# A two-layer encoder trunk: the last chunks of each down-projection product move into another buffer ring, and the last product ends in another order

## The chip, the cores and the metric

The kernel runs on one core of a Trainium2 chip. The metric is device time in microseconds (us), the median over several executions. The engines are TensorE (PE, with its weight loads as PEld), VectorE (DVE), ScalarE (ACT), GpSimd (POOL) and SyncE (SP), which issues the DMAs of this kernel.

## What is computed

An encoder trunk of two layers on 1024 tokens of width 1024, everything in float32. Each layer mixes tokens (windowed attention in the first, neighbourhood attention in the second, both beside heads that attend to 256 memory tokens), and then runs a gated feed-forward part. The change lies in the last two lines:

```python
gu = jnp.einsum('bsd,df->bsf', h, w_gu[i])
f = jnp.einsum('bsf,fd->bsd', jax.nn.silu(gu[..., :D_FF]) * gu[..., D_FF:], w_down[i])
x = x + rms_norm(f, norm_ffn_post[i])
```

D_FF is 2816, so the down projection multiplies a 1024x2816 matrix by a 2816x1024 one, and its rows are then scaled to unit mean square, multiplied by a gain and added to x.

## The kernel before

Every float32 operand is split into a high part that TensorE takes as it is (ScalarE copies it, L1118) and the rest (VectorE subtracts, L1120), and every product is three matmuls (`mm3`, L90 to L93): high x high, high x rest, rest x high.

The down projection is computed by blocks, two by two, with **seven products** of half size in place of eight, so that sums of blocks stand on either side. The sums are prepared in the gate and up stage and lie in HBM (`act_d`, `both_d`). Each product (`product4`, L1124) multiplies a 512x1408 block by a 1408x512 block: 11 chunks m of 128 inner rows, times four row tiles t, times three matmuls of 128x512, so 132 matmuls. The seven calls stand at the end of the stage; I number them 1 to 7 in program order. Products 2, 5, 6 and 7 end in a step on rows: `first_half`, `done_first` (L1157 adds, `part`, `finish`), `second_half`, `done_second`.

`operands` (L1103) gets chunk m: one DMA of 512 KB (L1117), or two of 256 KB (L1114, L1115), into a tile `draw`; then the high part `dh` on ScalarE (L1118) and the rest `dl` on VectorE (L1120). These tiles come from the pool `dp` with three buffers of each. In product 1 the first four chunks (`EARLY`) use `ring` instead, the pool through which the weights of the projections pass (two raw buffers `wr`, three of each part, `wh` and `wl`), because `dp` opens only when the stage before has ended.

`product4` runs chunks 0 to 8 with t inside. The last two (`GROUP`) are kept, and then run with t outside, so that the four accumulators end one after the other and `post(t)` follows each. PSUM holds eight accumulators, so the next product starts at once.

`part(t, k)` squares one half of a row tile on ScalarE with an accumulator (L1174) and multiplies the half by the gain on GpSimd (L1175). `finish(t, half)` adds the two sums of squares (L161), raises to the power -0.5 on GpSimd (L165), does one `scalar_tensor_tensor` on VectorE over 128x1024 (L1181) and stores the row tile (512 KB, L422 or L424). In the first layer it goes on with the next layer's norm; `turn_some` then transposes four row tiles on TensorE during product 6 (L186, eight matmuls of 128x128 each).

The order on each engine and on SP's queue is set by the framework: it takes instructions by priority, which is program order, as their inputs and buffers come ready by its own timing model, so that an instruction can stand ahead of earlier ones whose buffers are not free. Each queue then runs in that fixed order. The weights of the second layer's first projection come through `ring` too, after the down projection in program order (L105, L115, L116).

Of the kernel before, what the change touches and what calls it, by code (L numbers as in the profile page):

```python
# [12 lines left out]
ALU = mybir.AluOpType  # L13
# [10 lines left out]
HALF = 512  # L24
DFF = 2816
NF = DFF // P
FH = NF // 2
# [9 lines left out]
GROUP = 2  # L37
# [6 lines left out]
LEAD, EARLY = 6, 4  # L44
# [22 lines left out]
def build(nc, tc, ctx, x_in, mem_in, wts, t5, onehot, sinks, rpb, maskb, gains, out):  # L67
# [18 lines left out]
    dma = nc.sync  # L86
# [3 lines left out]
    def mm3(ps, lh, ll, rh, rl, start, stop):  # L90
        nc.tensor.matmul(ps, lh, rh, start=start, stop=False)  # L91
        nc.tensor.matmul(ps, lh, rl, start=False, stop=False)  # L92
        nc.tensor.matmul(ps, ll, rh, start=False, stop=stop)  # L93
# [14 lines left out]
    def unit_tiles(u, pl, n, tag=""):  # L108
        return [pl.tile([P, 1024], F32R, name=f"w{k}{u}", tag=f"w{k}{tag}", bufs=n) for k in "hl"]
# [48 lines left out]
    def rms(npool, parts):  # L158
        ms = npool.tile([P, 1], F32, name="ms", bufs=4)
        if len(parts) == 2:  # L160
            nc.vector.scalar_tensor_tensor(ms, parts[0], EPS, parts[1], ALU.add, ALU.add)  # L161
        else:
            nc.vector.tensor_scalar(ms, parts[0], EPS, None, ALU.add)
        r = npool.tile([P, 1], F32, name="r", bufs=4)
        nc.gpsimd.tensor_tensor(r, ms, mhalf, ALU.pow)  # L165
        return r

    def gain(npool, k, tag):
        g = npool.tile([P, D], F32, name=f"g_{k}", tag=tag)
        dma.dma_start(out=g, in_=gains[k:k + 1, :].broadcast_to([P, D]))  # L170
        return g
# [229 lines left out]
    def grid_rows(ap, j):  # L401
        return ap.rearrange("(r c) d -> c r d", c=COLS)[8 * j:8 * j + 8]
# [17 lines left out]
    def store_x(dst, t, i, grid):  # L420
        if grid:
            dma.dma_start(out=grid_rows(dst, i), in_=t)  # L422
        else:
            dma.dma_start(out=dst[i * P:(i + 1) * P, :], in_=t)  # L424
# [195 lines left out]
    for layer in range(DEPTH):  # L620
        windowed = layer == 0
        last = layer == DEPTH - 1
# [207 lines left out]
        gpost = gain(npool, DEPTH + layer, "g0")  # L830
# [48 lines left out]
        def load_xt(i):  # L879
            t = npool.tile([P, D], F32, name="xt", bufs=2)  # L880
            load_x(t, x_cur, i, layer == 0)
            return t
# [12 lines left out]
        for i in range(NT):  # L895
            accs = [psO.tile([P, HALF], F32, name="acc", tag="acc") for _ in range(2)]
            now_ao, ao = ao, heads_out(i + 1) if i < NT - 1 else None
            xt = load_xt(i)
# [75 lines left out]
        def add(o, a, b):  # L974
            nc.vector.tensor_tensor(o, a, b, ALU.add)  # L975
# [82 lines left out]
        for n, ((tH, tL), (b, t)) in enumerate(((T2, (1, 1)), (T1, (0, 0)), (T3, (0, 1)), (T4, (1, 0)))):  # L1058
            for i in range(4):
                eng = nc.gpsimd if (n, i) in TPOOL else nc.vector  # L1060
# [35 lines left out]
        x_next = out if last else x_scr[1]  # L1096
        held = []

        def turn_held():
            i, ht = held.pop(0)  # L1100
            turn(psD, "acc", ht, split_into(hH, hL, i))

        def operands(a, both, w):  # L1103
            def get(m):
                if a == 0 and m < EARLY:
                    raw = ring.tile([P, D], F32, name="draw", tag="wr", bufs=2)
                    h, lo = unit_tiles(f"d{m}", ring, 3)
                else:
                    raw = dp.tile([P, D], F32, name="draw", tag="draw", bufs=DRAW)
                    h, lo = (dp.tile([P, D], F32R, name=f"d{k}", tag=f"d{k}", bufs=DRAW) for k in "hl")  # L1110
                if both is None:
                    u = U_DN + NF * layer + m + (FH if w else 0)
                    ws = slice(HALF, D) if w == 2 else slice(0, HALF)
                    dma.dma_start(out=raw[:, :HALF], in_=act_d[layer][a, m])  # L1114
                    dma.dma_start(out=raw[:, HALF:], in_=wts[u, :, ws])  # L1115
                else:
                    dma.dma_start(out=raw, in_=both_d[layer][both, m])  # L1117
                nc.scalar.activation(h, raw, AF.Copy)  # L1118
                eng = nc.gpsimd if (both, m) in DPOOL else nc.vector
                eng.tensor_tensor(lo, raw, h.bitcast(F32), ALU.subtract)  # L1120
                return h, lo
            return get

        def product4(get, post, between=None, group=GROUP):  # L1124

            accs = [psD.tile([P, HALF], F32, name="acc", tag="acc") for _ in range(4)]

            def step(t, m, h, lo):
                ts = slice(t * P, (t + 1) * P)
                mm3(accs[t], h[:, ts], lo[:, ts], h[:, HALF:], lo[:, HALF:], m == 0, m == FH - 1)  # L1130

            kept = []
            for m in range(FH):
                hl = get(m)
                if m < FH - group:
                    for t in range(4):
                        step(t, m, *hl)
                else:
                    kept.append((m, hl))
                if between:  # L1140
                    between(m)
            for t in range(4):
                for m, hl in kept:
                    step(t, m, *hl)
                post(t, accs[t])
# [8 lines left out]
        tts, xts, sss = [], [], []  # L1154
# [12 lines left out]
                load_x(xt, x_new, 4 * half + t, False)  # L1167
                xts.append(xt)

        def part(t, k):  # L1170

            ks = slice(k * HALF, (k + 1) * HALF)
            junk = npool.tile([P, HALF], F32, name="junk", bufs=2)
            nc.scalar.activation(junk, tts[t][:, ks], AF.Square, scale=ROOT, accum_out=sss[t][:, k:k + 1])  # L1174
            nc.gpsimd.tensor_tensor(tts[t][:, ks], tts[t][:, ks], gpost[:, ks], ALU.mult)  # L1175

        def finish(t, half):
            i = 4 * half + t
            r = rms(npool, [sss[t][:, 0:1], sss[t][:, 1:2]])
            xt, tt = xts[t], tts[t]  # L1180
            nc.vector.scalar_tensor_tensor(xt, tt, r, xt, ALU.mult, ALU.add)  # L1181
            store_x(x_next, xt, i, last)
            if not last:
                ss = npool.tile([P, 1], F32, name="ss", bufs=4)
                nc.scalar.activation(tt, xt, AF.Square, scale=ROOT, accum_out=ss)
                r = rms(npool, [ss])
                nc.vector.scalar_tensor_tensor(tt, xt, r, gpre, ALU.mult, ALU.mult)
                held.append((i, tt))

        def first_half(t, ps):  # L1190
            add(tts[t][:, :HALF], ps, U[t])
            part(t, 0)

        def done_first(t, ps):
            add(tts[t][:, HALF:], ps, V[t])
            part(t, 1)
            finish(t, 0)

        def second_half(t, ps):
            if t == 0:  # L1200
                next_rows(1)
                load_xts(1)
            add(tts[t][:, HALF:], ps, V[t])
            add(U[t], ps, U[t])
            part(t, 1)

        def done_second(t, ps):
            add(tts[t][:, :HALF], ps, U[t])
            part(t, 0)
            finish(t, 1)  # L1210

        def turn_some(m):
# [2 lines left out]

        next_rows(0)
        product4(operands(0, None, 0), lambda t, ps: nc.scalar.activation(U[t], ps, AF.Copy))
        gpost = gain(npool, 4 * DEPTH + layer, "g0")
        product4(operands(1, None, 1), first_half)
        gpre = None if last else gain(npool, layer + 1, "g1")  # L1220
        load_xts(0)
        product4(operands(None, 3, None), lambda t, ps: add(U[t], ps, U[t]))
        product4(operands(None, 0, None), lambda t, ps: add(V[t], ps, U[t]))
        product4(operands(2, None, 2), done_first)
        product4(operands(None, 1, None), second_half, turn_some)
        while not last and held:
            turn_held()
        product4(operands(None, 2, None), done_second)
        dph.close()
        ops.close()  # L1230
        if last:
# [89 lines left out]
```

## Time and profile before

| | |
|---|---|
| median of 3 runs | 2269.01 us (2265.79 to 2272.14) |
| the profiled execution | 2261.95 us |
| its span, first to last instruction | 2260.2 us |
| mean granted TensorE clock in it | 0.983 of full |
| TensorE matmul busy | 2141.8 us, 95% |
| VectorE busy | 1513.8 us, 67% |
| ScalarE busy | 1064.9 us, 47% |
| GpSimd busy | 726.2 us, 32% |
| DMA, mean | 149 GB/s |

The down projection of the first layer lies at about 888 to 1112 us of the span, that of the second at 2020 to 2242 us. The 7 us between the profiled execution and the median lie outside the profile, so sums are made against 2261.95 us and moved to the median at the end.

### The profile page before, as it was taken

What the parts mean: (1) busy time and instruction counts of PE and PEld (TensorE: products, weight loads), DVE (VectorE), ACT (ScalarE), POOL (GpSimd) and SP (SyncE); (2) the same over time, 40 slices, a digit from 0 to 9 for tenths busy, and PEclk for the clock granted to TensorE, in tenths of its full rate; (3) what the DMA queues carried; (4) which work ended last, traced back from release to release, by engine and by line L of the source; (5) the groups of instructions that cost most, each with busy time, mean ns of one, the idle gap of its engine ahead of it and who ended that gap; (6) DMA issues with size and microseconds to landing.
All of it is one profiled execution on the core that took longest, in us unless ns stands there. A gap on an engine that the chain in (4) does not pass through costs nothing. (4 is left out here: it accounts for less than half of the span.)

```text
span 2260.2 us, 31296 instructions
## 1 busy us (share of the span) xinstructions
PE 2141.8 (95%) x10538; PEld 1779.4 (79%) x10538; DVE 1513.8 (67%) x2629; ACT 1064.9 (47%) x2162; POOL 726.2 (32%) x810
## 2 busy tenths in 40 slices
PE   7899888989999999999899999999899999999986
PEld 7678787768888888887788889777688888888865
DVE  5578785588777765556657665765877777755556
ACT  5488784442233333534457665754523333224333
POOL 3167661424333321102215342524233333211012
PEclk9999999999999999999999999999999999999998
DMA  6433445325555544856333232433255545446664
GB/s 206 118 88 91 135 135 156 98 79 189 175 183 170 180 138 162 276 193 235 114 104 97 78 87 69 132 112 107 75 180 183 184 170 177 145 146 222 193 207 164
DMA packets 152791, 336.49 MB, mean 149 GB/s; under 512 B 24727, under 2 KB 47127, under 8 KB 152632
## 3 DMA queue, kind: packets, MB, share of 16 engines
q1 hardware_dynamic: 152632, 334.50, 46.2%
q8 instruction: 84, 1.38, 0.3%
q14 instruction: 75, 0.61, 0.1%
HBM read 229.06 MB, written 95.03 MB: 143 GB/s over the span
## 5 line engine op out<-in xcount | busy, mean ns | idle before, releaser
L975 DVE TENSOR_TENSOR zt<-acc,zt 128x512 f32<-128x512 f32 x300 | 204.9, 686 | 155.9 <-PE acc L93 153.7
L1120 DVE TENSOR_TENSOR dl<-draw,dh 128x1024 fp32r<-128x1024 f32 x146 | 187.1, 1288 | 163.7 <-ACT dh L1118 163.1
L274 POOL TENSOR_TENSOR sn<-sn,st 128x384 f32<-128x384 f32 (+1 forms) x256 | 188.1, 736 | 254.3 <-DVE st L273 217.7
L1118 ACT ACTIVATE dh<-draw 128x1024 fp32r<-128x1024 f32 x146 | 154.0, 1059 | 218.5 <-PE acc L93 125.8
L92 PE MATMUL acc<-dl,dh 128*128 128x512 f32 x584 | 229.7, 393 | 14.9 <-DVE dl L1120 13.0
L93 PE MATMUL acc<-dh,dl 128*128 128x512 f32 x584 | 228.2, 391 | 0.0
L91 PE MATMUL acc<-dh 128*128 128x512 f32 x584 | 225.3, 391 | 1.3 <-ACT dh L1118 1.2
L918 ACT ACTIVATE gh<-zt 128x512 fp32r<-128x512 f32 x168 | 104.4, 628 | 175.7 <-PE acc L92 156.8
L994 POOL TENSOR_TENSOR tw<-tw 128x512 f32<-128x512 f32 x88 | 131.9, 1499 | 119.1 <-DMA tw<-in_wts 114.2
L1175 POOL TENSOR_TENSOR tt<-tt,g 128x512 f32<-128x512 f32 x32 | 52.2, 1643 | 363.9 <-ACT junk L1174 310.8
L116 DVE TENSOR_TENSOR wl<-wr,wh 128x1024 fp32r<-128x1024 f32 x92 | 118.2, 1285 | 67.3 <-ACT wh L115 65.5
L994 POOL TENSOR_TENSOR zt<-zt 128x512 f32<-128x512 f32 x66 | 90.3, 1368 | 205.1 <-DVE zt L972 201.7
L91 PE MATMUL psg<-hH,wh 128*128 128x512 f32 x384 | 153.1, 399 | 1.8 <-DVE k L229 1.4
L971 ACT ACTIVATE zt<-zt 128x512 f32<-128x512 f32 x84 | 53.1, 632 | 214.7 <-DVE zt L975 214.7
L115 ACT ACTIVATE wh<-wr 128x1024 fp32r<-128x1024 f32 x100 | 105.5, 1055 | 100.5 <-DMA wr<-in_wts 74.9
L92 PE MATMUL psg<-hL,wh 128*128 128x512 f32 x384 | 152.8, 398 | 0.0
L93 PE MATMUL psg<-hH,wl 128*128 128x512 f32 x384 | 152.5, 397 | 0.0
L292 PE MATMUL psv<-PT,v 128*128 128x256 f32 x656 | 143.0, 319 | 5.0 <-DVE attn L667 3.8
L98 DVE TENSOR_TENSOR PT<-pst,PT 128x384 fp32r<-128x384 f32 (+1 forms) x256 | 126.8, 495 | 29.7 <-ACT PT L97 25.1
L92 PEld LDWEIGHTS acc<-dl,dh 128*128 128x128 f32 x584 | 110.0, 188 | 43.3 <-DVE dl L1120 20.7
L272 ACT ACTIVATE sn<-sn,st 128x385 f32<-128x385 f32 (+3 forms) x192 | 113.0, 588 | 60.0 <-DVE st L269 55.7
L920 DVE TENSOR_TENSOR gl<-zt,gh 128x512 fp32r<-128x512 f32 x168 | 129.8, 775 | 7.5 <-ACT gh L918 7.5
(231 smaller groups left out, 5960.1 us busy)
## 6 DMA issues: line engine op xcount, KB each, us to landing
wr<-in_wts SPq DMA_DIRECT2D x146, 512.0 KB
draw<-both_d SPq DMA_DIRECT2D x88, 512.0 KB
both_d<-zt SPq DMA_DIRECT2D x88, 256.0 KB
tw<-in_wts SPq DMA_DIRECT2D x44, 512.0 KB
both_d<-tw SPq DMA_DIRECT2D x44, 512.0 KB
act_d<-zt SPq DMA_DIRECT2D x66, 256.0 KB
draw<-act_d SPq DMA_DIRECT2D x66, 256.0 KB
draw<-in_wts SPq DMA_DIRECT2D x66, 256.0 KB
```

Of the source, the lines that this page charges most:

```text
L91: nc.tensor.matmul(ps, lh, rh, start=start, stop=False)
L92: nc.tensor.matmul(ps, lh, rl, start=False, stop=False)
L93: nc.tensor.matmul(ps, ll, rh, start=False, stop=stop)
L98: nc.vector.tensor_tensor(ol, ps, oh.bitcast(F32), ALU.subtract)
L116: b = low[0].tensor_tensor(lo, raw, h.bitcast(F32), ALU.subtract)
L274: nc.gpsimd.tensor_tensor(sf, sf, rinv.broadcast_to([P, n]), ALU.mult)
L292: nc.tensor.matmul(pv[:, j % 2], pair.v(self.lo + c)[:, pair.vh + hh], self.PT[:, c], start=c == 0, stop=c == nk - 1)
L920: nc.vector.tensor_tensor(lo, src, h.bitcast(F32), ALU.subtract)
L975: nc.vector.tensor_tensor(o, a, b, ALU.add)
L994: nc.gpsimd.tensor_tensor(o, a, b, ALU.subtract)
L1118: nc.scalar.activation(h, raw, AF.Copy)
L1120: eng.tensor_tensor(lo, raw, h.bitcast(F32), ALU.subtract)
```

## The change

There are four edits, all in the down projection.

1. Chunks `m >= FH - held_back` use the ring's tiles. `held_back` is `GROUP` (chunks 9 and 10) for products 1 to 6 of both layers, 0 for product 7 of the first layer, and 3 (chunks 8 to 10) for product 7 of the second.
2. Product 7 of the second layer keeps five chunks rather than two for the end with t outside.
3. In that product the multiplication by the gain moves from GpSimd to VectorE.
4. In its `finish` the 128x1024 operation becomes two of 128x512, the second half of the row first, each followed by its own store of 256 KB.

```diff
-        def operands(a, both, w):
+        def operands(a, both, w, held_back=GROUP):
             def get(m):
-                if a == 0 and m < EARLY:
+                if (a == 0 and m < EARLY) or m >= FH - held_back:
                     raw = ring.tile([P, D], F32, name="draw", tag="wr", bufs=2)
                     h, lo = unit_tiles(f"d{m}", ring, 3)
                 else:
...
-        def part(t, k):
+        def part(t, k, eng=nc.gpsimd):
...
-            nc.gpsimd.tensor_tensor(tts[t][:, ks], tts[t][:, ks], gpost[:, ks], ALU.mult)
+            eng.tensor_tensor(tts[t][:, ks], tts[t][:, ks], gpost[:, ks], ALU.mult)
...
             xt, tt = xts[t], tts[t]
+            if last and half:
+                for k in (1, 0):
+                    ks = slice(k * HALF, (k + 1) * HALF)
+                    nc.vector.scalar_tensor_tensor(xt[:, ks], tt[:, ks], r, xt[:, ks], ALU.mult, ALU.add)
+                    dma.dma_start(out=grid_rows(x_next[:, ks], i), in_=xt[:, ks])
+                return
...
             add(tts[t][:, :HALF], ps, U[t])
-            part(t, 0)
+            part(t, 0, nc.vector if last else nc.gpsimd)
             finish(t, 1)
...
-        product4(operands(None, 2, None), done_second)
+        if last:
+            product4(operands(None, 2, None, 3), done_second, group=5)
+        else:
+            product4(operands(None, 2, None, 0), done_second)
```

## Rows read from the trace of the kernel before

**Rows 1.** The page: span, and busy time, share and instructions by engine.

```profile
span 2260.2 us, 31296 instructions
PE 2141.8 (95%) x10538; PEld 1779.4 (79%) x10538; DVE 1513.8 (67%) x2629; ACT 1064.9 (47%) x2162; POOL 726.2 (32%) x810
```

**Rows 2.** Stretches of the second layer: us, busy by engine, clock, DMA, GB/s.

```profile
2110.00:2160.00 50.00, 50.00 (x222) 41.41 (x221) 26.63 (x25) 19.94 (x19) 0.00 (x0) 1.00 0.63 196
...
2174.00:2180.00 6.00, 1.79 (x9) 1.16 (x8) 5.50 (x7) 1.67 (x3) 5.45 (x4) 1.00 0.41 104
```

**Rows 3.** Timeline of DVE: adds on last accumulators (start, us, idle before).

```profile
1008.76 0.69 DVE L1157 TENSOR_TENSOR v<-acc,u 128x512 f32<-128x512 f32 x1 [0.67 <-PE acc L93]
...
2111.71 0.69 DVE L1157 TENSOR_TENSOR u<-acc,u 128x512 f32<-128x512 f32 x1 [0.67 <-PE acc L93]
...
2141.63 0.69 DVE L1157 TENSOR_TENSOR v<-acc,u 128x512 f32<-128x512 f32 x1 [0.67 <-PE acc L93]
```

**Rows 4.** Timeline of PE in products 6 and 7 of both layers.

```profile
1053.48 1.03 PE L186 MATMUL pst<-ident,tt 128*128 128x128 f32 x8
...
1082.36 0.50 PE L92 MATMUL acc<-dl,dh 128*128 128x512 f32 x1 [2.66 <-DVE dl L1120]
...
1111.46 0.39 PE L93 MATMUL acc<-dh,dl 128*128 128x512 f32 x1
...
2174.07 1.07 PE L91 MATMUL acc<-dh 128*128 128x512 f32 x4
2179.35 0.50 PE L92 MATMUL acc<-dl,dh 128*128 128x512 f32 x1 [4.21 <-DVE dl L1120]
...
2241.88 0.39 PE L93 MATMUL acc<-dh,dl 128*128 128x512 f32 x1
```

**Rows 5.** Timeline of ACT and DVE: one chunk's split within product 4.

```profile
2136.19 1.06 ACT L1118 ACTIVATE dh<-draw 128x1024 fp32r<-128x1024 f32 x1 [1.66 <-PE acc L93]
...
2137.28 1.23 DVE L1120 TENSOR_TENSOR dl<-draw,dh 128x1024 fp32r<-128x1024 f32 x1 [1.49 <-ACT dh L1118]
```

**Rows 6.** Timeline of DVE where product 6 of the second layer begins.

```profile
2174.74 2.29 DVE L1181 SCALAR_TENSOR_TENSOR xt<-tt,r,xt 128x1024 f32<-128x1024 f32 x1
...
2178.08 1.21 DVE L1120 TENSOR_TENSOR dl<-draw,dh 128x1024 fp32r<-128x1024 f32 x1
...
2183.87 1.22 DVE L1120 TENSOR_TENSOR dl<-draw,dh 128x1024 fp32r<-128x1024 f32 x1
```

**Rows 7.** The chain that ended last, in product 6 of the second layer.

```profile
2179.36 7.12 DMA draw<-both_d
...
2201.10 9.38 DMA draw<-both_d
```

**Rows 8.** Timeline of SP's queue there.

```profile
2185.89 8.64 SPq L1117 DMA_DIRECT2D draw<-both_d  x3
```

**Rows 9.** Stretches in product 6, first layer, and product 1, second layer.

```profile
1066.00:1072.00 6.00, 5.83 (x31) 4.89 (x32) 3.68 (x5) 2.16 (x4) 0.00 (x0) 1.00 0.93 309
...
2040.00:2050.00 10.00, 9.24 (x41) 7.29 (x40) 4.90 (x4) 4.82 (x6) 0.00 (x0) 1.00 0.92 310
```

**Rows 10.** Timeline of ACT: the second layer's first weights in the ring.

```profile
923.98 1.06 ACT L115 ACTIVATE wh<-wr 128x1024 fp32r<-128x1024 f32 x1 [0.15 <-DMA wr<-in_wts]
```

**Rows 11.** Timeline of DVE, ACT and SP at the kernel's end.

```profile
2238.22 0.69 DVE L1157 TENSOR_TENSOR tt<-acc,u 128x512 f32<-128x512 f32 x1 [1.76 <-PE acc L93]
...
2239.49 0.19 ACT L1174 ACTIVATION_READ_ACCUMULATOR junk<-tt 128x1 f32 x1
...
2244.04 8.91 SPq L422 DMA_DIRECT2D out<-xt  x4
...
2249.09 1.22 DVE L161 SCALAR_TENSOR_TENSOR ms<-ssp 128x1 f32<-128x1 f32 x1
...
2251.03 1.29 DVE L1181 SCALAR_TENSOR_TENSOR xt<-tt,r,xt 128x1024 f32<-128x1024 f32 x1 [0.73 <-POOL r L165]
```

**Rows 12.** The last stretch of the span, columns as in rows 2.

```profile
2259.00:2260.20 1.20, 0.00 (x0) 0.00 (x0) 0.00 (x0) 0.00 (x0) 0.00 (x0) 0.50 0.00 0
```

## The prediction, made blind

> **What bounds the kernel now.** I read the page's busy times first: TensorE is busy 95% of the span [rows 1], so time can come only from the few places where it waits, or from the ends. The table of stretches then shows where. From 2110 to 2160 us TensorE is busy 50.00 of 50 us, with DVE at half of that [rows 2]: inside a product nothing is to be had. The adds that follow a last accumulator stand 2141.63 - 2111.71 = 29.92 us apart [rows 3]; that is one product, 132 matmuls of 0.227 us, 2.72 us per chunk. From 2174 to 2180 it is busy 1.79 of 6 us [rows 2].
>
> So I count what products 6 and 7 lose. In the second layer product 5 ends at 2141.63 + 29.92 = 2171.55, product 7 at 2241.88 + 0.39 = 2242.27 [rows 3, 4]: 70.7 us for 59.84 us of matmuls, **10.9 lost**. In the first layer they run from 1008.76 + 29.92 = 1038.68 to 1111.85, 73.2 us, with four groups of transposes of 1.03 us in them [rows 3, 4]: **9.2 lost**. The third place is the end: from 2242.27 to the span's end at 2260.2 TensorE has nothing left, **17.9 us**. 38 us in all.
>
> **The buffers (edit 1).** A chunk's split starts when the chunk three before it leaves TensorE. ACT starts at 2136.19, DVE ends at 2137.28 + 1.23 = 2138.51 [rows 5]: 2.32 us, and it is needed two chunks (5.44 us) after its start, a lead of 3.1 us. At a product's end this fails: chunks 9 and 10 hold two of three buffers for 24 matmuls, so the next product's chunk 1 can be split only in the last 0.7 us, when the work on finished rows has already filled DVE's queue. There an operation of 2.29 us at 2174.74 stands ahead of that chunk's subtraction at 2178.08 [rows 6]. TensorE has issued the four matmuls on its high part at 2174.07 and waits 4.21 us [rows 4]. The first layer's product 7 waits 2.66 us at its chunk 1 in the same way [rows 4]. The delay goes on: a raw buffer is free only after its subtraction, so the next loads go late, and then take 7.12 and 9.38 us on the chain [rows 7], beside stores and loads of row tiles.
>
> With chunks 9 and 10 in the ring, product 5's chunks 6, 7 and 8 leave TensorE at 2160.7, 2163.4 and 2166.1 (5.44 us before 2171.55, and 2.72 steps back). Three splits, 1.23 us of DVE each, fit before the adds begin at about 2168. The loads of chunks 3, 4 and 5 follow at about 2163 to 2168.5; before, chunk 4's was issued at 2179.36 [rows 7]. The 4.21 us go. What is late next is chunk 6: its load waits for chunk 3's subtraction, which may start at 2174.3 (chunk 0 leaves) but can again stand behind row work, say until 2179.3. With 7.12 us of load and 2.32 us of split it is ready at 2188.7; TensorE wants it at 2171.55 + 16.3 = 2187.9. With 9.38 us it is 3.1 us late. SP's queue can hold it longer: three loads spread over 8.64 us there, the loads waiting for buffers [rows 8]. So I leave 2.9 of 10.9 us and take **8.0 gained**, between 4.2 (only the first wait) and 10.9.
>
> In the first layer the same work carries the next norm and the transposes' splits, and DMA engines are 93% busy at 309 GB/s in product 6 [rows 9], so bandwidth keeps some of it late: **5.5 gained** of 9.2, between 2.7 (the wait at 1082.36) and 9.2.
>
> **What the ring costs.** In product 1 DMA is already 92% busy at 310 GB/s, and TensorE idles 0.76 of 10 us [rows 9]. Two ring loads that slip ahead are 1.05 MB, 3.4 us at that rate, per layer; or the spare buffers remove the 0.76. I take **1.0 lost** in each layer, nearer the idle that is there, between 0.8 gained and 3.4 lost. The second layer's first weights, split at 923.98 in the first layer's product 2 [rows 10], now wait for the ring until product 6 is through. I cost that at nothing: product 7 gives 30 us of cover, and three splits are 7 us. Without cover it is a load and a split, 9.4 + 2.3 = 11.7 us, once. Ring loads and splits standing earlier in SP's, ACT's and DVE's queues cost nothing as long as what queues behind keeps its lead of 3.1 us.
>
> **Five kept chunks (edit 2).** The matmuls are the same. With t outside, the four accumulators end 15 matmuls, 3.40 us, apart, not 1.36. Chunks 6 to 10 are wanted 0.68 us apart. Chunk 7 is split 2.32 us after chunk 4 leaves, while chunk 5 still runs (2.72). If the ring's three come after it, the last subtraction ends at 2.32 + 3.69 = 6.0 us, and is wanted at 5.7: 0.3 us. The ring has two raw buffers, so chunk 10's load must also wait for chunk 8's split. If that split is not moved ahead, the load of 7.12 us comes after it and TensorE stops for about 7 us. I take **0**, since the ring stands free from product 6's end, 14 us before; the bound is 7 lost.
>
> **The end (edits 3 and 4).** Now four rows queue on DVE and GpSimd after the accumulators end, and the last operation of DVE ends at 2251.03 + 1.29 = 2252.32, 10.05 us after TensorE. A two-element sum for a row's scale takes 1.22 us there and the row operation waits 0.73 us for GpSimd [rows 11]. With 3.40 us between rows and the gain on DVE, a row needs 0.69 + 0.69 + 0.15 + 0.73 (a wait that the next row's add can fill) + 2 x 0.65 = 3.6 us (an estimate for the halves, half of 1.29), so only the last row is left. From its add to the end of its square 2239.68 - 2238.22 = 1.46 [rows 11], the sum and the power 0.9, two halves 1.3: 3.7 us after TensorE, or 5.5 if 0.6 us per row piles up. I take 4.3: 5.7 gained. The last store goes from 2252.32 to 2260.2, 7.9 us, of which nothing moves in the last 1.2 [rows 12]; the four were issued over 8.91 us [rows 11], so they overlap. Half a store is left, with the other half 0.65 us ahead: between 5 us and 8.5 (one more issue), I take 7.0: 0.9 gained. Together **6.6**, between 3.9 and 9.2.
>
> The Trainium skill, "DMA: Bandwidth & Descriptors", section "Anatomy of one DMA", gives a fixed cost of about 2.0 us per DMA, whatever its size, plus its bytes at 436 GB/s. By it the last half store would take 2.6 us as an estimate, the end would gain 11.0 and the whole sum 22.5. The trace disagrees: 7.9 us for 512 KB, where the formula gives 3.2. The rule also speaks against halves, and is a rival below.
>
> **Sum:** 8.0 + 5.5 - 2.0 + 0 + 6.6 = 18.1 us. The profiled execution, 2261.95, becomes 2243.9; the median stands 7.06 us above it, so 2269.01 - 18.1 = **2250.9**. A measurement of this kernel can tell about 0.3%, 6.8 us.
>
> **The rivals.** (B) *The queue orders keep the row work ahead.* Only the two named waits go, loads stay late: 4.2 + 2.7 - 2.0 + 6.6 = 11.5, 2257.5. For it: 2.29 us operations and loads of 9 us remain; against it: three chunks are split before row work starts. (C) *The last product starves* on chunk 10's load: 18.1 - 7 = 11.1, 2258. Against it: weights were moved ahead by 190 us at 923.98 [rows 10]. (D) *Halved stores one after another*: four more fixed parts (the 1.2 us without traffic and some start, 2 us each) give 8 back, 2259. The page named above has the rule. The overlap in rows 11 speaks against it. (E) *It does not do what it says*: the splits still come where they came, since DVE's order puts them behind row work, and product 1 pays its 6.8: only the end is gained, 2269, no change. (F) *Slower.* A ring chunk's split is placed ahead on ACT and DVE by a model that expects its load sooner than it lands; everything behind it on both in-order queues waits. Twelve products carry such chunks. A wait w costs w - 3.1 each, so 5.5 us costs 2.4 x 12 = 29, against 18.1: 2280. It decides from w = 3.1 + 18.1/12 = 4.6. For it: landings of 7 to 9 us [rows 7]; against it: a free raw buffer is loaded a whole product early.
>
> **Chances.** Forecast 0.55 (its own range 2243 to 2258), B 0.20, C 0.08, D 0.02, E 0.08, F 0.07. Faster: 0.55 + 0.20 and most of C and D, 0.81; same: E and the rest of C and D, 0.12; slower: F, 0.07. The range goes from 2240, near all upper bounds, to 2263, which takes in B, C and D and leaves out E and F and a little.
>
> **What would show it.** Right: in product 6 of both layers no wait of TensorE at chunk 1, the subtractions of chunks 0 to 2 before the first add of product 5; products 6 and 7 in some 63 us in the second layer; from the last matmul to the span's end some 11 us. Wrong: subtractions of early chunks among the row operations (B, E); TensorE idle within the last product's t = 0 (C); idle under 1 us turned into waits of 2 us in products 2 to 4 with ACT waiting for a `draw` of the ring (F).

## The result, and the profile after

The changed kernel takes **2253.89 us** (median, 2251.45 to 2255.26); the kernel before, run beside it, 2267.86 (2265.79 to 2272.14). The ratio is 0.9938 with a 95% interval of 0.992 to 0.9955, so 14.0 us less, between 10.2 and 18.1. The profiled execution took 2251.45 us, the shortest of the four, and 10.5 less than the one of before; its page begins:

```profile
span 2249.6 us, 31265 instructions
PE 2143.0 (95%) x10538; PEld 1781.7 (79%) x10538; DVE 1511.8 (67%) x2637; ACT 1063.4 (47%) x2162; POOL 718.9 (32%) x806
```

TensorE does the same 10538 matmuls in the same busy time as in [rows 1]; the span around them is shorter. I cut both traces at the same instructions and compared lengths. Products 6 and 7 run from the last add of product 4 plus one product of 29.92 us to the last matmul. Ideal is 59.84 us, in the first layer 63.96 with its four transposes.

| stretch, us | before | after | gained |
|---|---|---|---|
| up to the first layer's down projection (code unchanged) | 887.65 | 890.83 | -3.18 |
| first layer, products 1 to 4 | 121.11 | 120.38 | 0.73 |
| first layer, products 6 and 7 | 73.17 | 67.97 | 5.20 |
| from there to the second layer's down projection | 908.53 | 907.55 | 0.98 |
| second layer, products 1 to 4 | 121.25 | 122.35 | -1.10 |
| second layer, products 6 and 7 | 70.72 | 67.57 | 3.15 |
| last matmul to DVE's last operation | 10.05 | 7.09 | 2.96 |
| DVE's last operation to the span's end | 7.85 | 6.02 | 1.83 |

The first row is a caution: its code is the same in every kernel of this study, and it took between 887.0 and 892.3 us in their profiles. So the spans of two profiles can be compared to some 5 us only, while a cut at the same instructions compares one stretch by itself. Without that row the gains come to 13.7 us, near the 14.0 of the medians.

**Where the first wait went.** DVE's timeline around the end of product 5 in the second layer, after the change (start, us, what, idle before it in brackets):

```profile
2159.13 1.23 DVE L1120 TENSOR_TENSOR dl<-draw,dh 128x1024 fp32r<-128x1024 f32 x1 [1.50 <-ACT dh L1118]
2161.85 1.23 DVE L1120 TENSOR_TENSOR dl<-draw,dh 128x1024 fp32r<-128x1024 f32 x1 [1.49 <-ACT dh L1118]
2164.57 1.23 DVE L1120 TENSOR_TENSOR dl<-draw,dh 128x1024 fp32r<-128x1024 f32 x1 [1.49 <-ACT dh L1118]
2165.71 1.28 DVE L1157 TENSOR_TENSOR tt<-acc,v 128x512 f32<-128x512 f32 x2
...
2169.07 2.31 DVE L1187 SCALAR_TENSOR_TENSOR xt<-tt,r,xt 128x1024 f32<-128x1024 f32 x1 [0.82 <-POOL r L165]
...
2172.11 2.31 DVE L1187 SCALAR_TENSOR_TENSOR xt<-tt,r,xt 128x1024 f32<-128x1024 f32 x1
...
2177.16 1.29 DVE L1187 SCALAR_TENSOR_TENSOR xt<-tt,r,xt 128x1024 f32<-128x1024 f32 x1 [0.44 <-POOL r L165]
2178.43 1.22 DVE L1120 TENSOR_TENSOR dl<-draw,dh 128x1024 fp32r<-128x1024 f32 x1
...
2189.36 1.23 DVE L1120 TENSOR_TENSOR dl<-draw,dh 128x1024 fp32r<-128x1024 f32 x1 [4.58 <-ACT dh L1118]
```

The subtractions of product 6's chunks 0, 1 and 2 now stand ahead of the first add. In [rows 6] chunk 1's stood at 2178.08, behind the row work; now chunk 3's stands there, at 2178.43. The same queue of row operations delays a chunk that is needed two chunks later. PE's timeline in the same stretch:

```profile
2179.71 0.80 PE L92 MATMUL acc<-dl,dh 128*128 128x512 f32 x1 [2.44 <-DVE dl L1120]
2180.30 0.63 PE L93 MATMUL acc<-dh,dl 128*128 128x512 f32 x1
2180.73 0.63 PE L91 MATMUL acc<-dh 128*128 128x512 f32 x1
...
2190.64 0.50 PE L92 MATMUL acc<-dl,dh 128*128 128x512 f32 x1 [0.76 <-DVE dl L1120]
```

A wait of 4.21 us at chunk 1 [rows 4] has become one of 2.44 at chunk 3 and smaller ones from chunk 6 on. The windows, with the columns of [rows 2]:

```profile
2110.00:2160.00 50.00, 50.00 (x222) 41.41 (x221) 26.15 (x24) 19.40 (x19) 0.00 (x0) 1.00 0.62 197
2174.00:2180.00 6.00, 3.56 (x16) 2.67 (x15) 5.21 (x6) 2.12 (x2) 4.43 (x3) 0.97 0.60 178
2180.00:2186.00 6.00, 6.00 (x21) 4.78 (x21) 4.69 (x4) 0.00 (x0) 0.06 (x1) 0.75 0.79 249
2186.00:2192.00 6.00, 5.24 (x23) 3.90 (x22) 1.23 (x1) 1.06 (x1) 0.00 (x0) 1.00 0.94 313
...
2192.00:2198.00 6.00, 4.72 (x20) 3.33 (x19) 2.45 (x2) 2.12 (x2) 0.00 (x0) 1.00 0.99 348
```

Of the 7.73 us that products 6 and 7 still lose, 2.44 + 0.76 + 1.28 = 4.5 are idle in these rows. Another 6.00 - 21 x 0.227 = 1.2 are matmuls that took longer: 21 of them in a full 6.00 us at a granted clock of 0.75. The starts of all matmuls in the trace place the whole. What exceeds 0.227 us from one start to the next comes to 4.3 us at chunk 3 (2.6 for the wait, 1.7 for the slower matmuls behind it), 1.2 at chunk 6, 1.8 at chunk 7 and 0.35 in product 7. SP's queue and ACT show why chunk 6 and its followers are late:

```profile
2177.56 0.32 SPq L418 DMA_DIRECT2D xt<-x_scr  x1
2178.47 0.61 SPq L422 DMA_DIRECT2D out<-xt  x1
2179.68 0.33 SPq L1117 DMA_DIRECT2D draw<-both_d  x1
2181.41 1.77 SPq L422 DMA_DIRECT2D out<-xt  x1
2183.28 2.54 SPq L1117 DMA_DIRECT2D draw<-both_d  x2
```

```profile
2188.27 1.06 ACT L1118 ACTIVATE dh<-draw 128x1024 fp32r<-128x1024 f32 x1 [10.13 <-DMA draw<-both_d]
```

Chunk 6's load is issued at 2179.68, among the second half's row loads and the first half's row stores, and ACT can take it at 2188.27, 8.6 us later.

**The end.** DVE's timeline over the last product's rows:

```profile
2226.33 0.69 DVE L1157 TENSOR_TENSOR tt<-acc,u 128x512 f32<-128x512 f32 x1 [3.00 <-PE acc L93]
2227.81 0.69 DVE L1175 TENSOR_TENSOR tt<-tt,g 128x512 f32<-128x512 f32 x1 [0.79 <-ACT junk L1174]
2228.42 0.15 DVE L161 SCALAR_TENSOR_TENSOR ms<-ssp 128x1 f32<-128x1 f32 x1
2229.24 1.42 DVE L1184 SCALAR_TENSOR_TENSOR xt<-tt,r,xt 128x512 f32<-128x512 f32 x2 [0.66 <-POOL r L165]
2230.57 0.69 DVE L1157 TENSOR_TENSOR tt<-acc,u 128x512 f32<-128x512 f32 x1
...
2239.15 0.68 DVE L1157 TENSOR_TENSOR tt<-acc,u 128x512 f32<-128x512 f32 x1
...
2242.17 1.41 DVE L1184 SCALAR_TENSOR_TENSOR xt<-tt,r,xt 128x512 f32<-128x512 f32 x2 [0.73 <-POOL r L165]
```

The last matmul ends at 2236.49. The two-element sum of 1.22 us of [rows 11] is down to 0.15, but two waits stand in every row: 0.79 us of the gain for ACT's square, 0.66 of the row operation for GpSimd's power. Nothing is placed in either, and the rows follow one another at 4.24 us (2226.33 to 2230.57) where accumulators come every 3.40. So the last row's add starts 2.66 us after TensorE has finished.

### The profile page after: what moved, and what is told of

It is laid out like the page before. It is cut to its first block, busy times and chain, and to the rows that moved or that the text cites. A ratio compares the mean times of both kernels' runs of the same rounds, so it can differ in the third digit from the quotient of the medians.

```text
span 2249.6 us, 31265 instructions
## 1 busy us (share of the span) xinstructions
PE 2143.0 (95%) x10538; PEld 1781.7 (79%) x10538; DVE 1511.8 (67%) x2637; ACT 1063.4 (47%) x2162; POOL 718.9 (32%) x806
## 4 chain that ended last, share of the span: by engine, by line
PE 72%; DVE 6%; ACT 5%; issue 5%; DMA 4%; POOL 3%; SPq 1%; POOLq 0%; DVEq 0%; ACTq 0%
PE acc L92 18%; PE acc L91 18%; PE acc L93 18%; PE psg L91 3%; PE psg L92 3%; PE psg L93 3%; PE psv L292 2%; PE pst L282 2%; PE pss L254 1%; PE pss L255 1%; POOL zh L853 1%; ACT sn L272 1%; DMA draw<-both_d 1%; DMA wr<-in_wts 1%; DMA draw<-in_wts 1%
## 5 line engine op out<-in xcount | busy, mean ns | idle before, releaser
L1120 DVE TENSOR_TENSOR dl<-draw,dh 128x1024 fp32r<-128x1024 f32 x119 | 148.5, 1257 | 133.6 <-ACT dh L1118 133.1
L1118 ACT ACTIVATE dh<-draw 128x1024 fp32r<-128x1024 f32 x119 | 125.3, 1058 | 172.9 <-PE acc L93 101.7
L92 PE MATMUL acc<-dl,dh 128*128 128x512 f32 x476 | 187.4, 394 | 8.8 <-DVE dl L1120 8.6
L91 PE MATMUL acc<-dh 128*128 128x512 f32 x476 | 186.2, 391 | 0.5 <-ACT dh L1118 0.5
L93 PE MATMUL acc<-dh,dl 128*128 128x512 f32 x476 | 185.9, 391 | 0.0
L1175 POOL TENSOR_TENSOR tt<-tt,g 128x512 f32<-128x512 f32 x28 | 45.8, 1652 | 334.3 <-ACT junk L1174 334.3
L282 PE MATMUL pst<-ident,sn 128*128 128x128 f32 x656 | 116.2, 277 | 8.2 <-POOL sn L274 4.5
```

The costliest lines, as they stand in the source:

```text
L282: nc.tensor.transpose(pt[:, c], self.sn[:, c * P:(c + 1) * P], ident)
```

## The experiments

Two questions were open: what still holds products 6 and 7 in the second layer, and what each part of the end is worth. "Below" is against the kernel before on the same chip, worked out from the ratio and that kernel's median: 2266.07 us for no_stores, late_rows and best, 2265.16 for the others. Stretches come from one profile of each run, cut as in the table above. Apart from end_only's, the intervals of all these ratios overlap that of the change (0.992 to 0.9955). So the medians do not clearly tell these kernels from the change, and what a part is worth is read from its stretch.

### The parts alone

**ring_only** keeps the last chunks in the ring and undoes the end:

```
-            part(t, 0, nc.vector if last else nc.gpsimd)
+            part(t, 0)
...
         if last:
-            product4(operands(None, 2, None, 3), done_second, group=5)
+            product4(operands(None, 2, None, 0), done_second)
```

with the halves block of `finish` removed as well.

> The ring in products 1 to 6 alone; product 7 of both layers and the end as before. Theory (the freed buffers carry a little over half of the gain): 7 to 10 us below the kernel before; from the end of product 5 to the end of product 7 about 68 us in both layers (70.7 and 73.2 before, 67.6 and 68.0 in the changed kernel); from the last matmul to the span's end 17.9 us as before. Rival (the wait only moves from chunk 1 to chunk 3, and the new end carries nearly all): 0 to 4 us below.

Measured: 2254.24 us, ratio 0.9961 (0.9949 to 0.9974), 8.8 us below (5.9 to 11.6 by its interval). Products 6 and 7 took 68.73 us in the second layer and 68.02 in the first; from the last matmul to the span's end 18.21, as before (17.90). The ring's gain lies in products 6 and 7: products 1 to 4 took 0.75 us less than before in the first layer and 1.9 more in the second. The end is independent of it.

**end_only** keeps the end and gives chunks 9 and 10 back to the common buffers:

```
-        def operands(a, both, w, held_back=GROUP):
+        def operands(a, both, w, held_back=0):
```

> The new end of the last product alone (three chunks in the ring, five kept, gain on VectorE, halves); products 1 to 6 as before. Theory: 4 to 6 us below the kernel before, 13.1 us from the last matmul to the span's end, products 6 and 7 losing what they lost before (10.9 and 9.2 us). Rival (the last product needs the ring of product 6 too, or starves on chunk 10): a wait of over 2 us within its kept chunks, and less than 2 us below.

Measured: 2262.68 us, ratio 0.999 (0.9979 to 1.0), at most 4.8 us below, where the theory had 4 to 6. The end took 13.15 us, as in the full change, and products 6 and 7 71.23 us in the second layer and 74.56 in the first, no less than before (70.72 and 73.17), with the wait back at its old place and size:

```profile
2187.51 0.79 PE L92 MATMUL acc<-dl,dh 128*128 128x512 f32 x1 [4.21 <-DVE dl L1120]
```

So each part makes its own stretch. But products 1 to 4 took 122.46 and 124.93 us in this profile, 1.35 and 3.68 more than before, which hid most of the end's gain. Part of it can be placed. Between 26 and 29 us into product 1 TensorE waits 1.01 + 0.76 us in the first layer and 1.97 + 0.76 in the second, where the kernel before waits 0.45 and 0.76 in all, and in the second layer a stretch follows that is in part at the lower of the clock's two levels (0.83 granted from 2050 to 2060). Why that wait is longer, with this part of the code unchanged, is not settled; it is not a starving last product.

### What the end is made of

**two_kept** holds two chunks of the last product back, not five, so that all four accumulators end nearly together:

```
-            product4(operands(None, 2, None, 3), done_second, group=5)
+            product4(operands(None, 2, None), done_second)
```

> The changed kernel with two kept chunks in the last product, not five. Theory (rows leave VectorE 4.24 us apart in the changed kernel, so accumulators 1.36 us apart pile up): the first add 4.1 us before the last matmul ends, four rows of 4.24 and 6 us of store, so some 19 us from the last matmul to the end, 5 to 6 us slower than the changed kernel, 8 to 9 below the kernel before. Rival (gain on VectorE and halves carry the end): within 1.5 us of the changed kernel.

Measured: 2251.16 us, ratio 0.9942 (0.9929 to 0.9954). The end took 15.59 us, only 2.5 more than with five: neither the theory's 5 to 6 nor the rival's 1.5, but nearer the rival. DVE's timeline shows why:

```profile
2231.64 0.68 DVE L1175 TENSOR_TENSOR tt<-tt,g 128x512 f32<-128x512 f32 x1
2232.24 0.15 DVE L161 SCALAR_TENSOR_TENSOR ms<-ssp 128x1 f32<-128x1 f32 x1
2232.39 0.69 DVE L1157 TENSOR_TENSOR tt<-acc,u 128x512 f32<-128x512 f32 x1
2233.05 1.41 DVE L1184 SCALAR_TENSOR_TENSOR xt<-tt,r,xt 128x512 f32<-128x512 f32 x2
```

Here the next row's accumulator is ready early, its add at 2232.39 is placed between the sum and the row operation, and no wait is left in this row; the four pairs of row operations start 2.7 us apart on the mean (2233.05 to 2241.21). Five kept chunks bring rows in one by one, and with that lose the work that filled the waits.

**own_tile** lets the gain write to a buffer that is free, not over the square's input:

```
-            eng.tensor_tensor(tts[t][:, ks], tts[t][:, ks], gpost[:, ks], ALU.mult)
+            to = U[t] if eng is nc.vector else tts[t][:, ks]
+            eng.tensor_tensor(to, tts[t][:, ks], gpost[:, ks], ALU.mult)
...
-                    nc.vector.scalar_tensor_tensor(xt[:, ks], tt[:, ks], r, xt[:, ks], ALU.mult, ALU.add)
+                    nc.vector.scalar_tensor_tensor(xt[:, ks], tt[:, ks] if k else U[t], r, xt[:, ks], ALU.mult, ALU.add)
```

> The changed kernel, but the product with the gain goes to a tile of its own in the last product, so it need not wait for the square that reads the same half. Theory (that wait, 0.79 us per row, is why rows take 4.24 us on VectorE against accumulators 3.40 us apart): rows under 3.6 us apart, the last add starts within 0.5 us of the last matmul's end instead of 2.6 us, and the end comes about 3 us earlier: 16 to 18 us below the kernel before. Rival (stores or GpSimd's power set the row's pace): rows still over 4 us apart, within 1 us of the changed kernel.

Measured: 2248.18 us, ratio 0.9934 (0.992 to 0.9947), the end 10.74 us, 2.4 less than with the change. DVE's timeline:

```profile
2232.69 0.68 DVE L1157 TENSOR_TENSOR tt<-acc,u 128x512 f32<-128x512 f32 x1
2233.40 0.69 DVE L1176 TENSOR_TENSOR u<-tt,g 128x512 f32<-128x512 f32 x1
...
2236.44 0.68 DVE L1157 TENSOR_TENSOR tt<-acc,u 128x512 f32<-128x512 f32 x1
...
2239.53 0.75 DVE L1185 SCALAR_TENSOR_TENSOR xt<-u,r,xt 128x512 f32<-128x512 f32 x1
```

The gain follows its add with no wait, rows are 3.63 to 3.75 us apart, and the last add starts 0.85 us after the last matmul (2235.59). The theory's 3.6, 0.5 and 3 us were each missed by a little. The 0.79 us were a write that waited for another engine's read.

**pool_gain** leaves the last product's gain on GpSimd (`part(t, 0)`).

> The changed kernel with the gain of the last product back on GpSimd. Theory (edit 3 as made costs: on VectorE a row waits for the square before the gain, for the power before the row operation, and nothing fills the waits): rows keep up with accumulators 3.40 us apart, the last add starts within 0.5 us of the last matmul's end, and from there to the span's end takes 11 to 12.5 us instead of 13.1. Rival (GpSimd beside VectorE stretches its operations, 2.3 us for 1.28 as in the kernel before): rows over 4 us apart, 13 us or more.

Measured: 2251.31 us, ratio 0.9941 (0.9923 to 0.996), the end 14.89 us, 1.8 more. The rival's numbers came, by another way than it said:

```profile
2230.69 0.69 DVE L1157 TENSOR_TENSOR tt<-acc,u 128x512 f32<-128x512 f32 x1
2232.23 0.16 DVE L161 SCALAR_TENSOR_TENSOR ms<-ssp 128x1 f32<-128x1 f32 x1 [0.85 <-ACT junk L1174]
2234.07 1.42 DVE L1184 SCALAR_TENSOR_TENSOR xt<-tt,r,xt 128x512 f32<-128x512 f32 x2 [1.69 <-POOL r L165]
2235.40 0.69 DVE L1157 TENSOR_TENSOR tt<-acc,u 128x512 f32<-128x512 f32 x1
```

DVE's operations take the same time as with the change. The row operation waits 1.69 us for the power, which GpSimd can start only after its own gain, and rows are 4.71 apart.

**whole_rows** scales and stores whole rows again (the halves block of `finish` removed).

> The changed kernel with whole rows in the last product: one operation of 1.28 us and one store of 512 KB per row. Theory: the last store starts 0.65 us later and takes 7 to 7.9 us instead of 6.0 after VectorE's end, so the end comes 0.5 to 1.9 us later. Rival (each store pays a fixed cost of its own, so halves cost): the end comes earlier by 0.5 us or more.

Measured: 2249.21 us, ratio 0.9933 (0.9918 to 0.9947), the end 13.92 us, 0.8 more: DVE's last operation comes 6.57 us after TensorE where halves take 7.09, and from there to the span's end it is 7.34 us where the last half needs 6.02.

### What still holds products 6 and 7

**first_gain_dve** takes GpSimd's multiplication away from beside the row operations, for the second layer's first half of the rows:

```
-            part(t, 1)
+            part(t, 1, nc.vector if last else nc.gpsimd)
```

> The changed kernel with the gain of product 5 of the second layer on VectorE too. Theory (GpSimd's multiplications pace the rows after product 5 and with them chunk 3's subtraction at 2178.43): the row operation falls from 2.31 to 1.3 us, chunk 3's subtraction ends 1.5 to 3 us earlier, the wait of 2.44 us at chunk 3 falls below 1 us, and products 6 and 7 lose about 5 us instead of 7.7. Rival (the loads of chunks 6 to 8, 8.6 and 9.6 us, set the end of product 6 anyway): the waits at chunks 6 to 8 grow by what the first loses, and the loss stays within 1 us of 7.7.

Measured: 2248.71 us, ratio 0.9928 (0.9909 to 0.9946). DVE, SP and ACT there, with product 5's end at 2166.72 (2168.92 with the change):

```profile
2169.48 1.28 DVE L1187 SCALAR_TENSOR_TENSOR xt<-tt,r,xt 128x1024 f32<-128x1024 f32 x1 [0.44 <-POOL r L165]
...
2173.37 1.22 DVE L1120 TENSOR_TENSOR dl<-draw,dh 128x1024 fp32r<-128x1024 f32 x1
...
2187.12 1.22 DVE L1120 TENSOR_TENSOR dl<-draw,dh 128x1024 fp32r<-128x1024 f32 x1 [6.26 <-ACT dh L1118]
```

```profile
2175.23 0.43 SPq L1117 DMA_DIRECT2D draw<-both_d  x1
```

```profile
2186.03 1.06 ACT L1118 ACTIVATE dh<-draw 128x1024 fp32r<-128x1024 f32 x1 [10.09 <-DMA draw<-both_d]
```

The row operation fell from 2.31 to 1.28 us, chunk 3's subtraction began 6.65 us after product 5's end where it took 9.51 with the change, and its wait was gone. Yet products 6 and 7 took 67.79 us, as with the change (67.57). Chunk 6's load was issued 8.51 us after product 5's end, 2.25 earlier than with the change (10.76), and could be used at 19.31, no earlier than there (19.35): the whole wait now stood at chunk 6. The rival held: DVE's queue was the first thing in the way, and the loads were right behind it.

**late_xt** moves the second half's row loads out of product 6, to chunk 2 of product 7, in both layers (the edit for the second is shown):

```
-                load_xts(1)
...
+            product4(operands(None, 2, None, 3), done_second, lambda m: load_xts(1) if m == 2 else None, group=5)
```

> The changed kernel with the second half's row tiles loaded during product 7, in both layers, not during product 6. Theory (four loads of 512 KB beside four stores lengthen the loads of chunks 6 to 8, 8.6 and 9.6 us): those land in 7 us or less, the three waits at chunks 6 to 8 of the second layer (1.03, 0.68 and 1.03 us) go, products 6 and 7 lose 5 us instead of 7.7 there and 1 us less in the first layer. Rival (the loads are late because they are issued late, behind the rows): the waits stay within 0.5 us.

Measured: 2248.66 us, ratio 0.9933 (0.9916 to 0.995). The first layer gained 1.4 (66.61 us), as the theory had it; the second did not (68.67). There chunk 6's load was issued at 2176.08, again 10.76 us after product 5's end (2165.32), and taken by ACT at 2186.44, 10.4 us later, with no row load near it and the stores still in their places; a weight load of the ring, at 2173.19, had taken the row load's place ahead of it. SP, then ACT:

```profile
2167.80 3.68 SPq L422 DMA_DIRECT2D out<-xt  x2
```

```profile
2186.44 1.06 ACT L1118 ACTIVATE dh<-draw 128x1024 fp32r<-128x1024 f32 x1 [11.91 <-DMA draw<-both_d]
```

Row loads are not what holds it.

**no_stores** leaves out the stores of the second layer's first four row tiles, half of the output:

```
-            store_x(x_next, xt, i, last)
+            if not last:
+                store_x(x_next, xt, i, last)
```

> The changed kernel without the stores of the first four row tiles of the second layer, so half of the output is not written. Theory (loads and stores go through one queue, so the load of chunk 6 stands behind up to 2 MB of stores, at 250 GB/s some 8 us, however early or late it is issued): chunk 6's load lands in 6 us or less, the waits at chunks 6 to 8 of the second layer go, only the 2.6 us at chunk 3 and its slow clock stay, and products 5's end to 7's end takes 63 to 65 us instead of 67.6. Rival (the load of chunk 6 is late because it is issued behind the row work): the waits at chunks 6 to 8 stay, 67 us or more.

Measured: 2247.64 us, ratio 0.9922 (0.9904 to 0.994). Products 6 and 7 took 62.68 us, 4.9 less than with the change. SP, then ACT:

```profile
2172.93 3.36 SPq L418 DMA_DIRECT2D xt<-x_scr  x2
...
2181.21 3.18 SPq L1117 DMA_DIRECT2D draw<-both_d  x2
```

```profile
2186.77 1.06 ACT L1118 ACTIVATE dh<-draw 128x1024 fp32r<-128x1024 f32 x1 [7.10 <-DMA draw<-both_d]
```

Chunk 6's load was issued at the same point, 10.76 us after product 5's end (2170.45), and could be used 5.6 us later, not 8.6 to 10.8. Three of the row loads even stood ahead of it here. Only the 2.44 us at chunk 3 stayed; behind it TensorE was full from 2186 to 2192 (6.00 of 6). Set beside late_xt this settles what holds the loads. In both, four transfers of 512 KB stand ahead of chunk 6's load, issued at the same times (2.5, 5.5, 7.9 and 9.6 us after product 5's end), and the third is the same weight load. The other three are stores there and row loads here. So it is not how much stands ahead, but that it is stores of finished rows, issued among the weights in the same queue.

**late_rows** keeps all stores, but issues them among the loads of product 7 (one behind each of chunks 0 to 3), and the row loads after them, in both layers:

```
+        def rows_late(m):
+            if m < 4:
+                tc.keep_in_program_order(store_x(x_next, *done[m], last))
+            if 3 <= m < 7:
...
+            product4(operands(None, 2, None, 3), done_second, rows_late, group=5)
```

> The changed kernel with the stores of the first half's row tiles and the loads of the second half's both moved into product 7, in both layers, in SP's queue between its loads. Theory (as for the run without stores): the second layer's products 6 and 7 take 63 to 65.5 us instead of 67.6, the first layer's 65 to 66.6 instead of 68.0, 14 to 20 us below the kernel before. Rival (the traffic only moves and makes product 7 wait): product 6 gains as above, product 7 gives it back in waits at its chunks 3 to 8, and the sums stay within 1 us.

Measured: 2254.03 us, ratio 0.9946 (0.9927 to 0.9964); products 6 and 7 took 69.13 us in the second layer, 1.6 more than with the change, and 67.67 in the first, where the theory had at most 66.6. In product 6 of the second layer only the wait at chunk 3 was left, and chunk 6's load could be used 5.1 us after its issue. Product 7 stopped in its turn: the rival held.

```profile
2184.75 0.50 PE L92 MATMUL acc<-dl,dh 128*128 128x512 f32 x1 [2.44 <-DVE dl L1120]
...
2218.61 0.79 PE L92 MATMUL acc<-dl,dh 128*128 128x512 f32 x1 [2.87 <-DVE dl L1120]
```

The profiled execution was the longest of five (2258.09 us), and its products 1 to 4 took 3.7 and 1.4 us more than with the change, which this edit does not touch; how much of that is in the median is not known.

**best** joins late_rows, first_gain_dve and own_tile.

> Three edits together on the changed kernel: rows stored and loaded in product 7 (both layers), product 5's gain on VectorE in the second layer, the last gain into a tile of its own. Theory (with the stores gone from product 6, the earlier subtraction of chunk 3 now counts): second layer 60.5 to 63 us from product 5's end to product 7's end, first layer 65 to 66.6, last matmul to span's end 10.7, some 22 to 26 us below the kernel before. Rival (the gains overlap or product 7 waits for its loads): 18 us or less.

Measured: **2245.27 us**, ratio 0.9911 (0.9895 to 0.9927), 20 us below the kernel before, between 16.5 and 23.8: the lowest median of all kernels here. Against the change (0.9938) the intervals overlap a little, between 0.992 and 0.9927; in the profiles products 6 and 7 of the second layer take 3.4 us less (64.20) and the end 2.6 less (10.56). The first layer's, with 67.78, stay as they were, where the theory had 65 to 66.6, and the total lies between the theory's 22 to 26 us and the rival's 18. Its windows in products 6 and 7 of the second layer:

```profile
2172.00:2178.00 6.00, 6.00 (x28) 4.92 (x27) 5.56 (x7) 2.55 (x4) 1.46 (x1) 1.00 0.29 85
...
2202.00:2208.00 6.00, 3.60 (x16) 2.68 (x15) 6.00 (x6) 3.88 (x8) 4.39 (x3) 0.99 0.69 280
```

TensorE is full where it idled before, and idles 2.40 us once in product 7. In the second layer the theory's 60.5 to 63 us were missed by that one wait.

## Why the prediction was right, and where it was off

The forecast of 2250.9 us stands 3 us from the measured 2253.89, inside the range; 14.0 us were gained of 18.1. Some of the nearness is luck. The kernel before took 2267.86 us in the comparison, 1.15 less than the 2269.01 that the sum started from, and products 1 to 4 came out 1.6 us better than their term. The sum put the median 7.06 us above the profiled execution; with the change it was 2.44 above, and the profiled executions are only 10.5 us apart. By its gain of 11.5 us rival B lies as near: the interval, 10.2 to 18.1, holds B inside and the forecast at its edge. So the totals do not decide between the two, and the stretches have to.

The freed buffers worked as described, and two of the four signs came in full: no wait at chunk 1 of product 6, and the subtractions of chunks 0 to 2 ahead of product 5's first add. The end came in part (13.1 us for "some 11"). The fourth, products 6 and 7 in some 63 us, did not come (67.57).

- **Second layer, products 6 and 7: forecast 8.0, measured 3.15.** This is the term that was mis-sized, below even its lower bound of 4.2. The step that failed is "what is late next". It named the right place, chunk 3's subtraction behind row work and then chunk 6's load, but put the end of that subtraction at 2179.3, 7.75 us after product 5's end at 2171.55 and in time for chunk 3. With the change it ended at 2178.43 + 1.22 = 2179.65, 10.73 us after product 5's end. Those 3.0 us of row work are a wait at chunk 3 (2.44), with 1.7 us of slower matmuls behind it that the step had no term for, and push every load behind it. The load itself, 7.12 to 9.38 us in the step, was 8.6. So chunk 6's split was done at 2189.36 + 1.23 = 2190.59, 21.7 us after product 5's end, where the step had 17.2 to 19.4. The bound failed for the same reason: it took a removed wait for a gain, while the work that had caused it went on to delay the next chunk that needed DVE. The size is no accident of one profile: in the six with both edits and this half of the code near to unchanged (the change, two_kept, own_tile, pool_gain, whole_rows, first_gain_dve) this stretch takes 67.4 to 67.9 us.
- **First layer: forecast 5.5, measured 5.20.** late_xt shows that 1.4 more lay in the row loads of that layer; in the kernels whose first layer is that of the change the stretch takes 67.3 to 68.1 us.
- **Product 1: forecast 1.0 lost in each layer.** Products 1 to 4 gained 0.73 in the first layer and lost 1.10 in the second, both within the bounds. Together 1.6 us better than the sum.
- **The second layer's first weights, costed at nothing.** The stretch between the layers' down projections is 907.55 for 908.53 us; nothing was paid.
- **Five kept chunks, costed at nothing.** The last product did not starve: TensorE is busy in all of the last 14.5 us before its last matmul ends, and two_kept puts five against two at 2.5 us of gain in the end, by one profile each.
- **The end: forecast 6.6, measured 4.8.** DVE ended 7.09 us after TensorE and not 4.3, beyond the 5.5 of the bound, though the sum of the end stayed within its own. The row was estimated at 3.6 us of DVE, and its wait of 0.73 was to be filled by the next row's add. It took 4.24 to 4.35: nothing fills that wait, since the next accumulator comes no earlier, and the wait of the gain for the square (0.79) was not seen. own_tile, without that second wait, ran at 3.63 to 3.75 and ended DVE 4.69 us after TensorE. The last store was the other way: 6.02 us for a forecast of 7.0.
- **The rivals.** B's picture (the named waits go, loads stay late) describes the second layer, where even its 4.2 was not reached, though not the first, where 5.20 stands against its 2.7. C and F did not happen: TensorE does not starve in the last product, and products 1 to 4 keep their length to 1.1 us. D is answered by whole_rows: in the profile halves are worth 0.8 us, which the medians cannot tell. E is answered by the order of the subtractions, and by ring_only, 8.8 us below.

The Trainium skill, "DMA: Bandwidth & Descriptors", section "Anatomy of one DMA — SWDGE (gpsimd) path", would have given the last half store 2.6 us, an estimate by its fixed part and rate. That section is about DMAs issued from GpSimd, which the prediction does not say, and these stores are issued from SP. The traces disagree with the size: 6.02 us pass from DVE's last operation to the span's end with the half, 7.34 with a whole row. They agree that halving saves only a small part: 1.32 us between the two, where the rate gives 0.6.

What remains open: why products 1 to 4 were longer in the profiles of end_only and late_rows; how the stores hold the loads (no run put them on another queue); and why a load that went out 2.25 us earlier, with the stores ahead of it earlier too, could be used no earlier.

## What to carry to other kernels

When buffers are freed so that early work gets ahead of a busy stretch, ask which piece is the first that does not get ahead, and price it by the whole queue in front of it, DMAs included; a removed wait is not a lower bound of the gain while what caused it is still there. A load's time from issue to landing depends on what is issued around it, so an earlier issue alone need not help; and stores that are moved back can hold the loads there: product 7 then waited 2.87 us in late_rows and 2.40 in best. And an operation that overwrites another engine's input waits for that engine: on a path that sets the end, a free buffer for the output was worth 2.4 us.

## What the runs showed of the hardware

- Issuing a load earlier did not bring it earlier. Counted from product 5's end, chunk 6's load was issued at 8.51 us in first_gain_dve and 10.76 with the change, and could be used at 19.31 and 19.35. In late_xt, with a ring load in the row load's place, it was used later still (21.12), which is not explained; without the stores at 16.32. From issue to use that is 8.6 to 10.8 us with stores ahead, and 5.6 in no_stores and 5.1 in late_rows and best without. DMA engines were 0.79 to 0.99 busy there with the change, at 249 to 348 GB/s. The Trainium skill, "DMA: Bandwidth & Descriptors", section "Queues, rings and completion order", says that each DMA engine takes the descriptors of a ring in their order; no run here shows the order within an engine. It would not by itself explain the first two: in first_gain_dve the same three stores and one row load stand ahead, and they too were issued 1.4 to 2.0 us earlier.
- The row operation of 128x1024 took 2.31 us with GpSimd multiplying beside it and 1.28 with that multiplication moved to DVE. With the change GpSimd multiplies from 2168.99 to 2170.29 us, and the row operation that starts at 2169.07 is the first of the long ones. The Trainium skill, "GPSIMD Engine Reference", section "1. Specifications", has GpSimd share its SBUF interfaces with VectorE, for DVE instructions with two SBUF inputs among others; this operation has two, and the runs agree.
- The matmuls after the wait of 2.44 us ran at the lower of the clock's two levels for a while: they start 0.43 us apart (2180.30 and 2180.73), not 0.23, and the stretch from 2180 to 2186 was granted 0.75. In no_stores, after a wait of the same length at the same chunk, the stretch 2180 to 2186 was granted 1.00. Counted from start to start, the wait and the matmuls behind it cost 4.3 us in one run and 2.7 in the other, and what decides between them is not shown.
